# A later turn for the key's product in a planned schedule, and a third tile for the sample's state

## The chip, the cores and the metric

One core of a Trainium2 chip runs the whole program. The metric is the device time of one execution in microseconds (us); smaller is better. The profiled execution is one such execution, and its rows are what this document reads.

## The reference, cut to what matters

One inference step of a one-layer encoder over 512 prompt tokens and 32 sample tokens, each of width 1024. RMSNorm is followed by one wide input projection, three recurrent mixers (Mamba-2, GLA, RWKV-7), a gated merge, cross attention over 256 memory tokens, and a final norm. The change touches the RWKV-7 mixer, which is, for each of 16 heads with a 64 by 64 state S:

```
S_t = S_{t-1} diag(w_t) - (S_{t-1} kk_t)(kk_t * a_t)^T + v_t k_t^T
o_t = S_t r_t                # k7 = k7 * (1 + (a - 1) * k_a) is the key that enters as k_t
```

Prompt tokens start from a zero state, sample tokens from a given state, and both final states are outputs.

## The kernel before

All 544 tokens lie along the free axis and channels on 128 partitions. The big projections are sums of three float32 products with 128 by 128 weight blocks (tiles wh and wl against uh and ul, results in PSUM tiles pd): a block of weights is loaded by DMA into wraw, split into wh by ScalarE and wl by VectorE, and used by 48 matmuls. These dense blocks are also the filler for TensorE while a recurrence waits.

The RWKV mixer runs in eight iterations, one for each pair of heads, called 0 to 7 here. Tokens are cut into chunks of 64: chunks 0 to 7 are the prompt, chunk 8 the sample. One iteration passes through these generators:

- rw_A (preparation): from k, r and the decay to scaled operands on VectorE, ScalarE and GpSimd. GpSimd forms a factor (bk<-bk,dpar, L299) and from it the key k7, which lies in tile ks (ks<-ks,bk, L284). VectorE then forms bee (sq<-bk,GC), the key's product ka (bk<-ks,bk), kae (rn<-bk,GC) and rk (rs<-rs,par,ks). GpSimd copies a half of bk (bk<-bk, L305).
- rw_B: transposes tokens (ptk, copied by ScalarE to tm and t and from there by DMA into NK), multiplies bk with AR on TensorE (pp, 36 matmuls), masks them into NK, and stores parts to DRAM.
- rw_I: 31 steps of a small triangular inverse on GpSimd (im and td, 62 instructions).
- rw_J: two further block products of the inverse on TensorE (pW, then pT) with the ScalarE copy W between them.
- rw_C: the state chain, over chunk 8 first and then 0 to 7. In each chunk TensorE multiplies the state (pc<-Sb,AR), VectorE adds (R), TensorE solves (pc<-R,TT), VectorE writes NK (copy_predicated, L1198), TensorE multiplies again (pc<-NK), and VectorE updates the state (Sb<-Sb,GC,pc, or a plain copy in chunk 0, which has no state to start from).
- rw_N: the norm of the outputs.

Sb is a list of three tiles. The start state of the sample is loaded into Sb[2]. The new state of chunk c goes to Sb[c % 2], so chunk 8 writes Sb[0], which is also stored by DMA to the output (out_rwkv_s), and chunk 0 writes Sb[0] next.

The order of the instructions on every engine is fixed when the program is built. A planner (class Sched) keeps an estimated clock for every engine and an estimated finish for every region of a tile. Its generators run by priority; each appends instructions until it yields. A yielded number sends the generator to sleep until the planned clock of TensorE has advanced by that many nanoseconds; a yielded function, until it is true. `S.free("v")` is true once the planned VectorE is less than 900 ns ahead of TensorE; `S.at(x)` is the planned time that is left until x is written, on TensorE's clock, and zero when it is past. The chip does not see these clocks: it keeps the order and waits on semaphores. So a yield decides what stands ahead of an instruction in its engine's queue, not when it runs. The dense generator has the lowest priority and takes every turn that the others leave.

Many instructions come from helpers, and carry their lines: L284 is tensor_tensor, L293 scalar_tensor_tensor, L299 tensor_scalar, L305 copy, L278 activation, L245 matmul, L242 transpose, L327 DMA.

Of the kernel before, what the change touches and what calls it, by code (L numbers as in the profile page):

```python
# [46 lines left out]
       ("a", "v"): 145.0, ("a", "p"): 170.0, ("v", "a"): 130.0, ("v", "p"): 155.0, ("p", "v"): 70.0, ("p", "a"): 65.0,  # L47
       ("a", "q"): 150.0, ("v", "q"): 150.0, ("p", "q"): 150.0, ("v", "v"): 127.0, ("a", "a"): 153.0, ("p", "p"): 102.0}

W = dict(HOLD1=0, HOLD2=8, CALM=3000, EARLY1=1, DEPTH1=3, EARLY2=2, FAIR=1500, GRAIN=5, IS=900.0, IE=0, NQ=3000, XL=2, SG=6, PRW=800.0, R2=0.0, DE=2500.0, T2=0, FA=900.0, XM=3000.0, WARM=12)  # L50


class Cols:
# [72 lines left out]
class Sched:  # L126
# [22 lines left out]
    def run(self):  # L149
        idle = 0  # L150
        while self.threads:
# [4 lines left out]
            th = next(ready, None)  # L156
            if th is not None and th[0] >= 0 and self.n_small > W["FAIR"]:
                th = next((x for x in ready if x[0] == 9), th)
# [181 lines left out]
def body(tc, I, O):  # L340
    nc = tc.nc
    S = Sched(nc)
# [17 lines left out]
    with tc.manual_schedule(), \  # L360
# [447 lines left out]
        Sb = [rwp.tile([128, 2, 64], F32, name=f"Sb{i}") for i in range(3)]  # L808
# [80 lines left out]
        def ch(a):  # L889
            return a.rearrange("p (c t) -> p c t", t=64)  # L890
# [4 lines left out]
        def rw_A(p):  # L895
# [51 lines left out]
            bk = rwp.tile([128, 9, 3, 64], F32, name="bk", tag="bk")  # L947
# [35 lines left out]
            k7 = ks  # L983
# [3 lines left out]
            ar = d["AR"]  # L987
# [13 lines left out]
            bee = sq  # L1001
            gcol = d["GC"]
            S.cp(gcol, EE[:, :, 64:65])
            S.tt(ch(bee), be, gcol.to_broadcast([128, 9, 64]), MUL)
            yield S.free("v")
            S.tt(ka, ch(k7), Gi, MUL)
            yield S.free("v")
            kae = rn
# [9 lines left out]
        def rw_B(p):  # L1018

            yield has(f"rwK{p}", "rwR", f"vs{p}")  # L1020
            rk, vs, kae, bee, bk, d = hand.pop(p)
            ar = d["AR"]
            rwr = pools["rwR"][1]
            nk = d["NK"]

            def tokens(n_, src):

                yield S.at(src)
                ps = yield from bank("ptk")
                for i in range(4):  # L1030
                    S.mm(ps[:, i * 128:(i + 1) * 128], src[:, i * 128:(i + 1) * 128], C("ident"), True, True, transpose=True)
                tm = rwr.tile([128, 4, 128], F32, name="tm", tag="tm", bufs=TMB)
                yield S.since(tm, 1, "a") - S.t["pe"]
                S.act(tm.rearrange("p c t -> p (c t)"), ps[:, :512], AF.Copy)
                for i in range(2):
                    h = 64 * i
                    g = h if n_ == 2 else 64 - h
                    for r in range(2):
                        S.store(out=nk[g:g + 64, r:8:2, i, 1 if n_ else 3, :], in_=tm[r * 64:r * 64 + 64, :, h:h + 64])
                yield S.free("a")  # L1040

            yield from tokens(0, vs)

            yield S.at(bk, ar)
            for c0, cn in ((0, 4), (4, 4), (8, 1)):
                ps = []
                for _ in range(2):
                    ps.append((yield from bank("pp")))
                for c in range(cn):
                    for i in range(2):  # L1050
                        hs = slice(64 * i, 64 * i + 64)
                        S.mm(ps[i][:, c * 128:c * 128 + 128], bk[hs, c0 + c, i:i + 2, :].rearrange("p a t -> p (a t)"),
                             ar[hs, c0 + c], True, True)
                for i in range(2):
                    S.tt(nk[:, c0:c0 + cn, i, 0:3:2, :], ps[i][:, :cn * 128].rearrange("p (c a t) -> p c a t", c=cn, a=2),
                         two(C("m_rw")[:, 64 * i:64 * i + 128]).unsqueeze(1).to_broadcast([128, cn, 2, 64]), MUL)
                yield S.free("v")
            for i in range(2):
                S.store(out=rows64(n_scr[p % 2], i), in_=nk[i * 64:i * 64 + 64, :, i, 2 * i, :])
            done.add(f"rwN{p}")  # L1060

            r2 = rwp.tile([128, 2, TP], F32R, name="r2", tag="r2")
            rh, rl = r2[:, 0], r2[:, 1]
            parts(rk[:, :T], rh[:, :T], rl[:, :T])
            yield S.at(rl[:, :T], vs)
            for (o, w) in HV:
                ps = yield from bank("pbn")
                head_sums(ps[:, :w], rh[:, o:o + w], rl[:, o:o + w])
                S.tt(rk[:, o:o + w], ps[:, :w], vs[:, o:o + w], MUL)
                yield S.free("v")  # L1070
            S.store(out=b_scr[p], in_=rk[:, :T])
            done.add(f"rwB{p}")
            yield from tokens(1, kae)
            yield from tokens(2, bee)
            ps = yield from bank("ptk")
            for n_, (src) in enumerate((kae, vs, bee)):
                S.mm(ps[0:64, n_ * 128:n_ * 128 + 128], src[:, 512:576], C("ident"), True, True, transpose=True)
            t8 = rwr.tile([64, 3, 128], F32, name="t8", tag="tm", bufs=TMB)
            yield S.since(t8, 1) - S.t["pe"]
            S.act(t8.rearrange("p c t -> p (c t)"), ps[0:64, :384], AF.Copy)  # L1080
            for i in range(2):
                h = 64 * i
                S.store(out=nk[64 - h:128 - h, 8, i, 1:4:2, :], in_=t8[:, 0:2, h:h + 64])
                S.store(out=nk[h:h + 64, 8, i, 1, :], in_=t8[:, 2, h:h + 64])
            done.add(f"rwA{p}")
# [66 lines left out]
        IE = "pv"[W["IE"]]  # L1152
# [11 lines left out]
        def rw_C(p):  # L1164

            d = slot[p % NSLOT]
            yield has(f"rwA{p}")
            for i in range(2):
                S.dma(out=Sb[2][64 * i:64 * i + 64, i], in_=I["s0_rwkv"][64 * i:64 * i + 64, p])
            yield has(f"rwI{p}")  # L1170
            AR, NK, TTt, GC = (d[n_] for n_ in ("AR", "NK", "TT", "GC"))
            st_ = None
            yield S.stored(NK)
            yield S.at(Sb[2], NK, TTt)
            for c0, cn in ((4, 5), (0, 4)):
                ps = yield from bank("pr")
                for c in range(cn):
                    for i in range(2):
                        hs, gs = slice(64 * i, 64 * i + 64), slice(64 - 64 * i, 128 - 64 * i)
                        S.mm(ps[hs, c * 64:c * 64 + 64], NK[gs, c0 + c, i, 2 * i, :], NK[gs, c0 + c, i, 3, :], True, True)  # L1180
                S.act(NK[:, c0:c0 + cn, 0, 0, :], ps[:, :cn * 64].rearrange("p (c t) -> p c t", t=64), AF.Copy)
            NB = blocks8(NK)
            for c in [8] + list(range(8)):
                Ss = Sb[2] if c == 8 else (None if c == 0 else st_)


                pa = yield from bank("pc")
                pb = yield from bank("pc")
                pu = pa[:, 128:256]
                VU, R = NK[:, c, :, 3, :], both(NK[:, c, 0, 0, :])  # L1190
                if Ss is not None:
                    S.mm(pa[:, 0:128], AR[:, c].rearrange("p a t -> p (a t)"), Ss, True, True)
                    r_ = rwp.tile([128, 2, 64], F32, name="R", tag="R")
                    S.tt(r_, two(pa[:, 0:128]), R, ADD)
                    R = r_
                yield S.at(NK[:, c, 0, 0, :] if Ss is None else R)
                S.mm(pu, TTt[:, c, :], R, True, True)
                nc.vector.copy_predicated(VU, two(C("blk1").bitcast(I32)), two(pu))  # L1198
                S.note("v", 203, (VU,), (pu,))
                yield S.at(VU)  # L1200
                for i in range(2):
                    S.mm(pb[:, i * 64:i * 64 + 64], NK[:, c, i, 1 - i:3 - i, :].rearrange("p a t -> p (a t)"), VU[:, i, :], True, True)
                ns = Sb[c % 2]
                for i in range(2):
                    hs = slice(64 * i, 64 * i + 64)
                    if Ss is None:
                        S.cp(ns[hs, i], pb[hs, hs])
                    else:
                        S.stt(ns[hs, i], Ss[hs, i], GC[hs, c, :], pb[hs, hs], MUL, ADD)
                    if c >= 7:  # L1210
                        S.store(out=O["rwkv_s" if c == 8 else "rwkv_p"][hs, p], in_=ns[hs, i])
                st_ = ns
                yield S.at(ns)
                S.act(NB[:, c, 3:8:4, :], two(pb[:, 0:128]), AF.Copy)
                if Ss is not None:
                    S.act(NB[:, c, 0:7:6, :], two(pa[:, 0:128]), AF.Copy)
                else:
                    nc.gpsimd.memset(NB[:, c, 0:7:6, :], 0.0)
                    S.note("p", 200, (NB[:, c, 0:7:6, :],), ())
            done.add(f"rwC{p}")  # L1220
# [914 lines left out]
```

## Time and profile before

| what | value |
|---|---|
| median of three runs | 1309.08 us (1308.45 to 1312.62) |
| profiled execution | 1309.37 us |
| its span, first to last instruction | 1307.6 us |
| TensorE busy | 1266.1 us, 97% of the span |
| VectorE busy | 841.5 us, 64% |
| ScalarE busy | 624.7 us, 48% |
| GpSimd busy | 356.9 us, 27% |
| mean granted TensorE clock | 0.986 |

Busy times of different engines overlap. A granted clock of 1.00 is 2.4 GHz and one of 0.50 is 1.2 GHz; a figure between is the mean of a stretch that has both. The profiled execution's time is 1.8 us more than its span.

### The profile page before, as it was taken

The page shows a single profiled execution, that of the slowest core. Times are in us where ns is not written, and L with a number is a line of the kernel's source. Part 1 is how long each engine was busy: PE and PEld are TensorE (multiplying, and loading weights), DVE is VectorE, ACT ScalarE, POOL GpSimd, SP SyncE. Part 2 cuts the span into 40 slices and gives each one's busy share as a digit, 9 for nine tenths or more (in the row PEclk, how much of TensorE's full clock was granted, in tenths as well). Part 3 has the DMA queues.
Part 4 walks back from the last instruction along what each step waited for, and adds up shares of the span by engine and source line. Part 5 has one row for each costly group of instructions (what it writes and reads, how often), then busy time and mean ns, then how long its engine had stood idle before and what let it go on. Part 6 is the DMA issues. An engine that isn't in the chain of part 4 may idle for free.

```text
span 1307.6 us, 27538 instructions
## 1 busy us (share of the span) xinstructions
PE 1266.1 (97%) x10848; PEld 1219.7 (93%) x10848; DVE 841.5 (64%) x1666; ACT 624.7 (48%) x1191; POOL 356.9 (27%) x706
## 2 busy tenths in 40 slices
PE   8999989998999999999999999999999999999997
PEld 8999989998999888999999999888999999999997
DVE  6857875767685967554464878676665756575543
ACT  6565445455556363444555463634445323444422
POOL 0014845818372846520010533132000000000000
PEclk8999989999999998999999999999999999999999
DMA  8644455353535353633532442363886445440302
GB/s 293 194 121 117 121 140 124 104 135 114 125 93 141 105 132 111 161 108 131 173 136 70 138 125 95 111 187 98 289 317 239 137 133 189 171 146 25 106 17 69
DMA packets 170385, 181.11 MB, mean 139 GB/s; under 512 B 100480, under 2 KB 123104, under 8 KB 170128
## 3 DMA queue, kind: packets, MB, share of 16 engines
q1 hardware_dynamic: 169824, 178.68, 44.7%
q8 instruction: 86, 1.41, 0.4%
q10 hardware_dynamic: 432, 0.67, 0.2%
q14 instruction: 43, 0.35, 0.1%
HBM read 136.27 MB, written 35.39 MB: 131 GB/s over the span
## 4 chain that ended last, share of the span: by engine, by line
PE 56%; DVE 6%; POOL 5%; ACT 2%; DMA 2%; issue 2%; SPq 0%; POOLq 0%; DVEq 0%; ACTq 0%
PE pd L245 43%; PE pc L245 3%; POOL im L284 2%; POOL td L284 2%; PE psc L245 1%; PE pO L245 1%; PE py L245 1%; PE pov L245 1%; DVE wl L284 1%; PE pp L245 1%; PE ph L245 1%; PE pS L245 1%; PE pss L245 1%; PE pT L242 1%; ACT L278 0%
## 5 line engine op out<-in xcount | busy, mean ns | idle before, releaser
L245 PE MATMUL pd<-ul,wh 128*128 128x272 f32 (+1 forms) x1632 | 437.3, 296 | 0.0
L245 PE MATMUL pd<-uh,wh 128*128 128x272 f32 (+1 forms) x1632 | 432.5, 294 | 0.2 <-ACT wh L278 0.2
L245 PEld LDWEIGHTS pd<-ul,wh 128*128 128x128 f32 (+1 forms) x1632 | 309.3, 190 | 3.9 <-issue 2.2
L245 PEld LDWEIGHTS pd<-uh,wh 128*128 128x128 f32 (+1 forms) x1632 | 309.0, 189 | 3.8 <-issue 1.8
L245 PE MATMUL pd<-uh,wl 128*128 128x272 f32 (+1 forms) x1632 | 254.5, 293 | 3.0 <-DVE wl L284 3.0
L245 PEld LDWEIGHTS pd<-uh,wl 128*128 128x128 f32 (+1 forms) x1632 | 222.0, 190 | 6.9 <-DVE wl L284 4.2
L284 DVE TENSOR_TENSOR wl<-wraw,wh 128x1024 fp32r<-128x1024 f32 (+1 forms) x143 | 177.7, 1245 | 39.3 <-ACT wh L278 36.1
L278 ACT ACTIVATE wh<-wraw 128x1024 fp32r<-128x1024 f32 (+1 forms) x143 | 149.8, 1048 | 64.2 <-PE pd L245 38.0
L245 PE MATMUL pd<-uh,wr 128*128 128x256 f32 (+1 forms) x768 | 148.7, 291 | 1.4 <-ACT uh L278 1.4
L284 POOL TENSOR_TENSOR im<-td,nd 108x84 f32<-108x84 f32 (+23 forms) x248 | 117.5, 474 | 88.8 <-DMA td<-in_eye 48.2
L245 PEld LDWEIGHTS pd<-uh,wr 128*128 128x128 f32 x768 | 121.1, 188 | 2.9 <-ACT uh L278 1.6
L284 POOL TENSOR_TENSOR td<-td,im 108x84 f32<-108x84 f32 (+23 forms) x248 | 107.3, 433 | 19.4
L284 POOL TENSOR_TENSOR macc<-macc,hrs 128x288 f32<-128x288 f32 x3 | 2.3, 799 | 378.0 <-DVE macc L293 378.0
L245 PE MATMUL pd<-ul,wr 128*128 128x256 f32 (+1 forms) x384 | 100.5, 293 | 0.1
L245 PEld LDWEIGHTS pd<-ul,wr 128*128 128x128 f32 x384 | 72.4, 189 | 1.5 <-issue 0.8
L278 ACT ACT_TABLE_LOAD x55 | 70.6, 1283 | 1.4 <-DVE tB L284 0.5
L278 ACT ACTIVATE fg<-pd 128x272 f32<-128x272 f32 x64 | 24.9, 394 | 84.7 <-PE pd L245 79.8
L293 DVE SCALAR_TENSOR_TENSOR Sb<-Sb,GC,pc 64x64 f32<-64x64 f32 x128 | 35.7, 279 | 35.7 <-PE pc L245 33.7
L278 ACT ACTIVATE lerpA<-pd,par 128x272 f32<-128x272 f32 x50 | 24.3, 487 | 68.5 <-PE pd L245 56.4
L245 PE MATMUL pc<-NK 128*128 128x64 f32 x288 | 43.2, 273 | 5.8 <-DVE NK L1198 3.4
L278 ACT ACTIVATE NK<-pc 128x128 f32<-128x128 f32 x136 | 30.3, 273 | 37.9 <-DVE Sb L293 34.3
L278 ACT ACTIVATE fg<-pd,dpar 128x272 f32<-128x272 f32 x48 | 23.2, 486 | 50.2 <-PE pd L245 36.8
(469 smaller groups left out, 2421.0 us busy)
## 6 DMA issues: line engine op xcount, KB each, us to landing
wraw<-in_wall SPq DMA_DIRECT2D x165, 512.0 KB
g_mg<-fg SPq DMA_DIRECT2D x24, 272.0 KB
mgt<-g_mg SPq DMA_DIRECT2D x24, 272.0 KB
NK<-tm SPq DMA_DIRECT2D x96, 64.0 KB
ab<-acs_d SPq DMA_DIRECT2D x8, 512.0 KB
nd<-n_scr SPq DMA_DIRECT2D x24, 144.0 KB
n_scr<-NK SPq DMA_DIRECT2D x16, 144.0 KB
TT<-d_scr SPq DMA_DIRECT2D x16, 144.0 KB
```

What stands on the lines that cost most here:

```text
L242: self.nc.tensor.transpose(out, lhsT, rhs)
L245: self.nc.tensor.matmul(out, lhsT, rhs, start=start, stop=stop, skip_group_check=shared)
L278: self.nc.scalar.activation(out=out, in_=in_, func=f, scale=scale, bias=bias)
L284: eng.tensor_tensor(out=out, in0=a, in1=b, op=op)
L293: self.nc.vector.scalar_tensor_tensor(out=out, in0=a, scalar=s, in1=b, op0=op0, op1=op1)
```

## The change

Four edits. A new constant KM is 1500 ns. In rw_A the turn that was given up after bee is given up ahead of bee, and in its old place, ahead of ka, the generator sleeps until TensorE's planned clock is 1500 ns past the planned finish of k7 (or 1500 ns, if k7 is planned to be finished already). In rw_B the sleep ahead of the pp products is 1500 ns longer. In rw_C chunk 8 writes its new state to Sb[2] in place of Sb[0], over the start state that it has just read. No arithmetic instruction is added, removed or resized.

```
-W = dict(..., XM=3000.0, WARM=12)
+W = dict(..., XM=3000.0, WARM=12, KM=1500.0)
...
             gcol = d["GC"]
             S.cp(gcol, EE[:, :, 64:65])
+            yield S.free("v")
             S.tt(ch(bee), be, gcol.to_broadcast([128, 9, 64]), MUL)
-            yield S.free("v")
+            yield S.at(k7) + W["KM"]
             S.tt(ka, ch(k7), Gi, MUL)
             yield S.free("v")
             kae = rn
...
             yield from tokens(0, vs)
-            yield S.at(bk, ar)
+            yield S.at(bk, ar) + W["KM"]
             for c0, cn in ((0, 4), (4, 4), (8, 1)):
...
-                ns = Sb[c % 2]
+                ns = Sb[c % 2 if c < 8 else 2]
```

## Rows read from the trace of the kernel before

**Rows 1.** Windows: busy us (and count) of each engine, granted TensorE clock, DMA.
```profile
core 0: us, PE busy (x) PEld busy (x) DVE busy (x) ACT busy (x) POOL busy (x), PEclk, DMA share, GB/s
100.00:640.00 540.00, 516.38 (x4891) 495.32 (x4890) 355.45 (x743) 266.15 (x547) 273.97 (x574) 0.98 0.45 123
...
177.40:182.30 4.90, 4.90 (x51) 4.59 (x53) 4.14 (x6) 0.21 (x1) 1.73 (x3) 0.50 0.83 241
...
323.90:330.90 7.00, 7.00 (x42) 6.45 (x43) 4.52 (x12) 1.95 (x5) 5.14 (x17) 0.60 0.44 114
...
510.70:518.20 7.50, 7.49 (x44) 6.92 (x46) 3.49 (x8) 0.51 (x3) 2.76 (x8) 0.56 0.50 141
```

**Rows 2.** Waits of TensorE, 85 to 640 us: us in total, times, longest.
```profile
PE pc L245 <- DVE R L284: 5.4, 6, 2.6
PE pc L245 <- DVE Sb L293: 4.9, 2, 3.6
PE pT L245 <- ACT W L278: 3.5, 1, 3.5
...
PE pp L245 <- DVE lerpA L819: 1.0, 1, 1.0
...
PE pc L245 <- DVE Sb L305: 0.4, 1, 0.4
```

**Rows 3.** Waits of VectorE over the whole span.
```profile
DVE bk L284 <- POOL ks L284: 5.8, 2, 3.9
...
DVE Sb L305 <- DMA out_rwkv_s<-Sb: 1.6, 2, 1.3
```

**Rows 4.** Timeline of VectorE, iteration 4: start, length, instruction, [idle before].
```profile
316.75 0.30 DVE L1198 COPY_PREDICATED NK<-con,pc 128x128 f32<-128x128 int32 x1
320.95 0.76 DVE L284 TENSOR_TENSOR bk<-ks,bk 128x576 f32<-128x576 f32 x1 [3.90 <-POOL ks L284]
321.63 1.68 DVE L284 TENSOR_TENSOR wl<-wraw,wh 128x1024 fp32r<-128x1024 f32 x1
323.24 0.56 DVE L293 SCALAR_TENSOR_TENSOR Sb<-Sb,GC,pc 64x64 f32<-64x64 f32 x2
...
325.12 0.28 DVE L284 TENSOR_TENSOR R<-pc,NK 128x128 f32<-128x128 f32 x1
```

**Rows 5.** Timeline of GpSimd, iteration 4.
```profile
317.26 1.35 POOL L284 TENSOR_TENSOR yr<-yr,bo 128x544 f32<-128x544 f32 x1
318.60 0.82 POOL L299 TENSOR_SCALAR bk<-bk,dpar 128x576 f32<-128x576 f32 x1
319.50 1.41 POOL L284 TENSOR_TENSOR ks<-ks,bk 128x576 f32<-128x576 f32 x1
```

**Rows 6.** Timeline of TensorE, iteration 4.
```profile
314.35 0.38 PE L245 MATMUL pc<-Sb,AR 128*128 128x128 f32 x2
...
316.33 0.38 PE L245 MATMUL pc<-R,TT 128*128 128x128 f32 x2
...
323.86 0.79 PE L245 MATMUL pc<-Sb,AR 128*128 128x128 f32 x2 [3.59 <-DVE Sb L293]
```

**Rows 7.** Timeline of VectorE, iteration 7.
```profile
508.12 1.87 DVE L284 TENSOR_TENSOR bk<-ks,bk 128x576 f32<-128x576 f32 x1 [1.88 <-POOL ks L284]
510.02 0.44 DVE L293 SCALAR_TENSOR_TENSOR fg<-fg,pd 128x272 f32<-128x272 f32 x1
510.37 0.28 DVE L284 TENSOR_TENSOR R<-pc,NK 128x128 f32<-128x128 f32 x1
```

**Rows 8.** Timeline of TensorE, iteration 7.
```profile
506.64 0.38 PE L245 MATMUL pc<-Sb,AR 128*128 128x128 f32 x2
...
510.71 0.80 PE L245 MATMUL pc<-R,TT 128*128 128x128 f32 x2 [2.62 <-DVE R L284]
```

**Rows 9.** Tile bk: durations in ns, min/median/max, over the eight iterations.
```profile
L299 POOL TENSOR_SCALAR bk<-bk,dpar x8: 817/1073/2456, 96.9 to 505.8; 128x576 f32<-128x576 f32 x8
L284 POOL TENSOR_TENSOR ks<-ks,bk x8: 1406/1422/2279, 98.7 to 506.7; 128x576 f32<-128x576 f32 x8
```

**Rows 10.** Timeline of ScalarE, 168 to 180 us: the copy ahead of W.
```profile
176.58 0.48 ACT L278 ACTIVATE t<-ptk 64x384 f32<-64x384 f32 x1 [2.75 <-DMA NK<-tm]
```

**Rows 11.** Timeline of TensorE, 575 to 590 us: end of iteration 7's inverse, start of its chain.
```profile
579.90 0.69 PE L245 MATMUL pT<-TT,W 32*32 32x32 f32 x32
587.79 1.26 PE L245 MATMUL pr<-NK 64*64 64x64 f32 x36
```

More of the change, by code (lines that the diff above doesn't have):

```diff
@@ L48 @@
        ("a", "q"): 150.0, ("v", "q"): 150.0, ("p", "q"): 150.0, ("v", "v"): 127.0, ("a", "a"): 153.0, ("p", "p"): 102.0}
-W = dict(HOLD1=0, HOLD2=8, CALM=3000, EARLY1=1, DEPTH1=3, EARLY2=2, FAIR=1500, GRAIN=5, IS=900.0, IE=0, NQ=3000, XL=2, SG=6, PRW=800.0, R2=0.0, DE=2500.0, T2=0, FA=900.0, XM=3000.0, WARM=12)
+W = dict(HOLD1=0, HOLD2=8, CALM=3000, EARLY1=1, DEPTH1=3, EARLY2=2, FAIR=1500, GRAIN=5, IS=900.0, IE=0, NQ=3000, XL=2, SG=6, PRW=800.0, R2=0.0, DE=2500.0, T2=0, FA=900.0, XM=3000.0, WARM=12, KM=1500.0)
 class Cols:
@@ L1003, in rw_A @@
             S.cp(gcol, EE[:, :, 64:65])
+            yield S.free("v")
             S.tt(ch(bee), be, gcol.to_broadcast([128, 9, 64]), MUL)
-            yield S.free("v")
+            yield S.at(k7) + W["KM"]
             S.tt(ka, ch(k7), Gi, MUL)
@@ L1042, in rw_B @@
             yield from tokens(0, vs)
-            yield S.at(bk, ar)
+            yield S.at(bk, ar) + W["KM"]
             for c0, cn in ((0, 4), (4, 4), (8, 1)):
@@ L1202, in rw_C @@
                     S.mm(pb[:, i * 64:i * 64 + 64], NK[:, c, i, 1 - i:3 - i, :].rearrange("p a t -> p (a t)"), VU[:, i, :], True, True)
-                ns = Sb[c % 2]
+                ns = Sb[c % 2 if c < 8 else 2]
                 for i in range(2):
```

## Prediction

> **What bounds the kernel now.** I read the windows first, then the waits of TensorE and VectorE, then the timelines around the longest waits. In the stretch from 100 to 640 us, where the eight RWKV iterations run, TensorE is busy for 516.4 of 540 us [rows 1]. So TensorE is the bound there, and what an edit can win is in its 23.6 us of gaps and in the stretches in which its clock is granted at half. The waits say where the gaps lie: 4.9 us behind the state update Sb, 3.6 us of it at once; 5.4 us behind R, 2.6 us at once; 3.5 us in one wait for W [rows 2].
>
> Sb and R run on VectorE, so the next question is what VectorE did before them. It waited for GpSimd's key only twice, for 5.8 us together, the longer time for 3.9 us [rows 3]. The reader is to see that these two waits and the two longest TensorE gaps behind Sb and R are the same events. In iteration 4 VectorE is free at 317.05 (316.75 + 0.30) and stands before ka until 320.95, because GpSimd ends k7 at 320.91 (319.50 + 1.41) [rows 4, 5]. Behind ka in VectorE's queue wait a split wl and the state update Sb; Sb runs only at 323.24 [rows 4]. TensorE reaches the product with that state at 320.27 (323.86 - 3.59) and stands for 3.59 us [rows 6]. In iteration 7 VectorE waits 1.88 us, ka then takes 1.87 us, and R, queued behind it, starts at 510.37; TensorE stands for 2.62 us before the solve that reads R [rows 7, 8].
>
> Each gap costs twice. After the first the granted clock is 0.60 in the mean of the next 7.0 us, after the second 0.56 in 7.5 us, which mixes the levels 1.2 and 2.4 GHz; before both gaps TensorE was doing dense products without a break [rows 1]. If work goes in proportion to the clock, 7.0 x 0.40 = 2.8 us and 7.5 x 0.44 = 3.3 us of TensorE's time are lost there. So the two events cost 3.59 + 2.8 + 2.62 + 3.3 = 12.3 us.
>
> **The turn ahead of ka.** Nothing is added to any engine; the order changes. Before, only VectorE's planned backlog was asked for, so ka was appended while its input was still being made. Now at least 1500 ns of TensorE's planned time lie between bee and ka, and what the other generators append in that time stands ahead of ka.
>
> Iteration 4: TensorE's next steps were due within that time, so wl and Sb go first. VectorE does them from 317.05: 1.68 + 0.56 us [rows 4], ending at 319.3, before TensorE is there at 320.27. The 3.59 us gap and its 2.8 us go. What is late next is R, which now stands behind ka. GpSimd's k7 ends at 320.91 at best; at worst the wl beside it stretches it from 1.41 to the longest in the eight, 2.28 us [rows 9], to 321.8. With ka's 0.76 us and R's 0.28 us [rows 4], R ends between 322.0 and 322.8. TensorE wants it 1.98 us after its state product (316.33 - 314.35) [rows 6], at 322.25. So 0 to 0.6 us of wait comes back. I take 0.6, since GpSimd's operations in these rows do stretch.
>
> Iteration 7: fg and R go ahead of ka, so the solve is not held. ka starts at 508.12 as before and takes 0.76 [rows 4] to 1.87 us [rows 7], ending between 508.9 and 510.0. Late next is the predicated write after the solve: the state product is at 506.64 [rows 8], the solve 2.0 us later, its write at about 509.0. It is 0 to 1.0 us late. I take 1.0, as ka was as slow as that in this very place. Both returns are taken without a fall of the clock, which these rows show behind gaps of 2.6 and 3.6 us.
>
> In the other six iterations VectorE did not wait at ka [rows 3], so there the new turn wins nothing.
>
> **The turn ahead of pp.** VectorE's instruction before pp kept TensorE's pp waiting for 1.0 us once [rows 2]. With 1500 ns more between them that goes: -1.0 us, between 0 and -1.0. Everything after it is up to 1.5 us later, and with ka's turn up to 3.0 us in an iteration: the masks in NK, the stores and reloads that feed the inverse, GpSimd's 62 instructions, pW and pT, and SyncE's queue of the same transfers. I cost this at nothing. The work that hides it is dense filler, which TensorE has for this stretch [rows 1], and the start of the next state chain: in iteration 7 pT ends at 580.59 and the chain's first product starts at 587.79 [rows 11], 7.2 us later. If that cover were gone, the last chain would start up to 3.0 us later, once, since earlier delays are taken up by the chain that is still running. Bounds 0 and +3.0; I take 0.
>
> **The sample's state in Sb[2].** Chunk 0's copy no longer waits until the store of chunk 8's state has read Sb[0]: VectorE lost 1.6 us in two such waits [rows 3], and TensorE lost 0.4 us behind that copy [rows 2]. The same instructions run otherwise. The reload of Sb[2] for the next iteration must now wait for that store, but a whole chain of eight chunks lies between. -0.4 us, between 0 and -1.6.
>
> **Sum.** -12.3 + 0.6 + 1.0 - 1.0 - 0.4 = -12.1 us against the profiled 1309.37 us: 1297.3. That execution lies 0.3 us above the median shown, so 1297 for a median. A change under 0.3%, 3.9 us, can't be told from none for this kernel.
>
> **Rivals.**
>
> *GpSimd becomes later, so part of the wait stays.* While VectorE stood before ka, GpSimd ran alone. Now VectorE works beside it. The same factor took 0.82 us then and up to 2.46 us elsewhere, k7 1.41 and up to 2.28 us [rows 5, 9]: together 1.64 + 0.87 = 2.5 us later. In iteration 4 k7 is then at 323.4 and R at 324.4, 2.2 us late, and with the low clock's 2.8 us 5.0 of the 6.4 us come back: 1297.3 - 0.6 + 5.0 = 1301.7. If iteration 7 goes the same way, ka ends at 511.4, 2.4 us late, and with 3.3 us for the clock: 1301.7 - 1.0 + 5.7 = 1306.4. For it: the spread of these durations. Against it: in iteration 4 the order puts only one wl and a short Sb beside them. The Trainium skill speaks for this rival ("SBUF — State Buffer", section "SBUF: two separate sides"): an operation of VectorE with two SBUF inputs and a GpSimd operation that reads SBUF exclude each other for a whole instruction, instead of sharing. By that rule one wl of 1.68 us could set k7 back by 1.68 us rather than 0.87, which by the steps above makes 1.4 us of the 0.6 and 1298.1 of the sum; the trace agrees that the same GpSimd work takes up to three times as long at some places (2.46 against 0.82 us).
>
> *The gaps only move.* The sleep is measured on planned clocks, and GpSimd ran later than ka's place in the order assumed, by 3.9 us in iteration 4 [rows 3]; 1.5 us is less. Also, a different order after iteration 0 changes what meets what in all later ones. If two gaps like those removed appear elsewhere, the time is 1307 to 1311. Against it: the instructions that TensorE missed were the next to be appended, so a small shift is enough.
>
> *A slower kernel: the inverse's copy W held behind a transposed tile.* Once, ScalarE stood 2.75 us before the copy t, because DMAs still read the tile's buffer, and W was queued behind [rows 10]; TensorE stood for 3.5 us before pT [rows 2] and then ran 4.9 us at 0.50 [rows 1]: 3.5 + 2.45 = 6.0 us a time. The transposes of rw_B come later now, and so closer to the next inverse product. Two further such meetings cancel the gain (1309.3); from the third on the kernel is slower: -12.1 + 18.0 = +5.9, 1315.3. Against it: it happened once in eight iterations.
>
> **How the numbers follow.** The forecast has a chance of 0.50, with its own range 1290 to 1301. The first rival has 0.18 (1302 to 1306), the second 0.16, the slower one 0.16. Faster by over 0.3%, below 1305.2: 0.50 and 0.15 of the first rival, 0.65. Within 0.3%: the rest of it and the second, 0.19. Slower: 0.16. The range: at the low end the W gap is broken up by the new order too and nothing comes back, 1297.3 - 6.0 - 1.6 = 1289.7, so 1289. At the high end it holds both middle cases, 1311, and leaves out the slower one and a little below.
>
> **What would show it.** After: no wait of VectorE for GpSimd's key above 2 us with Sb or R queued behind it; wl and Sb ahead of ka in iteration 4, fg and R in iteration 7; no TensorE wait of over 2 us behind Sb or R; two low-clock stretches fewer; TensorE's gaps in the RWKV stretch down from 23.6 us to about 16; no wait of chunk 0's copy for the store. I am wrong if new waits of some microseconds stand before W, pp or another link, each with a low-clock stretch behind it, or if GpSimd's factor and key take over 2 us each.

## The result, and the profile after

The changed kernel takes 1315.91 us in the median of nine runs (1313.18 to 1321.01), the kernel before 1308.07 us (1304.44 to 1312.62): a ratio of 1.0057, with a 95% interval of 1.0039 to 1.0076. It is slower, and outside the predicted range. In a second session of runs the same program had 1.0024 (1.0008 to 1.0041), so its cost is 0.2 to 0.6%. The profiled execution took 1321.0 us, the slowest of the nine, with a span of 1319.2 us.

Windows of the changed kernel, cut so that they part the start, the RWKV iterations, the stretch behind them and the tail (columns as in [rows 1]):

```profile
0.00:100.00 100.00, 93.48 (x705) 91.74 (x706) 65.52 (x115) 62.99 (x103) 5.46 (x28) 0.95 0.62 199
100.00:640.00 540.00, 513.48 (x4846) 489.79 (x4845) 357.51 (x744) 264.56 (x545) 279.89 (x580) 0.98 0.45 122
640.00:1010.00 370.00, 364.67 (x2989) 348.12 (x2988) 243.79 (x444) 186.71 (x320) 73.86 (x96) 1.00 0.49 164
1010.00:1400.00 390.00, 299.53 (x2315) 292.38 (x2313) 174.61 (x364) 111.03 (x225) 2.29 (x3) 0.99 0.27 90
```

The same windows of the kernel before, but for the one in [rows 1]:

```profile
0.00:100.00 100.00, 95.53 (x722) 93.57 (x723) 67.53 (x118) 63.47 (x104) 7.54 (x29) 0.97 0.62 199
...
640.00:1010.00 370.00, 366.34 (x3021) 350.14 (x3020) 248.07 (x450) 188.31 (x320) 73.08 (x101) 1.00 0.51 167
1010.00:1400.00 390.00, 287.87 (x2222) 280.72 (x2220) 170.45 (x358) 106.75 (x220) 2.30 (x3) 0.99 0.26 84
```

Both programs run the same matmuls, so the last row is a balance: what TensorE has not done by 1010 us it does in the tail. The tail's busy time is 299.53 against 287.87 us, 11.7 us more, and the span is 11.6 us longer. The matmuls missing at each cut tell where: 17 by 100 us, 45 more by 640, 32 more by 1010. In the RWKV stretch TensorE was idle for 26.5 us instead of 23.6. The profile of the second session (span 1313.2 us) has 23.7 us there, as before, 2 matmuls fewer at the start, and 40 fewer between 640 and 1010, where its idle time is 6.25 us against 3.66. So the expected 12 us are missing in both, and where the loss lies differs.

Did the waits go that the change is about? Waits of VectorE over the whole span, answering to [rows 3]:

```profile
DVE x L1134 <- DMA TT<-d_scr: 6.5, 5, 4.0
...
DVE bk L284 <- POOL ks L284: 1.4, 2, 0.8
```

The wait for GpSimd's key fell from 5.8 to 1.4 us, and chunk 0's wait for the store is no longer listed. But there is a new first row: the wait for the reloaded inverse (TT<-d_scr) is 6.5 us; before it was 3.1 us, 1.8 at the longest. Waits of TensorE from 85 to 640 us, answering to [rows 2]:

```profile
PE pc L245 <- DVE NK L1199: 9.3, 4, 3.6
PE pc L245 <- DVE R L284: 8.6, 12, 1.7
PE pT L245 <- ACT W L278: 3.4, 1, 3.4
PE pp L245 <- POOL bk L305: 1.4, 1, 1.4
```

Sb is not among the waits of 0.4 us and more, and the longest wait for R is 1.7 us. In their place stand 9.3 us for NK, 3.6 at once. Iteration 4 shows both halves of this. Timeline of VectorE, answering to [rows 4]:

```profile
316.81 0.57 DVE L293 SCALAR_TENSOR_TENSOR Sb<-Sb,GC,pc 64x64 f32<-64x64 f32 x2
318.16 0.76 DVE L284 TENSOR_TENSOR bk<-ks,bk 128x576 f32<-128x576 f32 x1 [0.79 <-POOL ks L284]
...
327.17 0.29 DVE L284 TENSOR_TENSOR R<-pc,NK 128x128 f32<-128x128 f32 x1 [0.94 <-PE pc L245]
331.46 0.95 DVE L1134 STREAM_TRANSPOSE x<-TT 64x256 f32<-64x256 f32 x2 [4.00 <-DMA TT<-d_scr]
332.44 1.29 DVE L284 TENSOR_TENSOR NK<-pp,con 128x512 f32<-128x512 f32 x2
333.64 0.29 DVE L1199 COPY_PREDICATED NK<-con,pc 128x128 f32<-128x128 int32 x1
```

and of TensorE, answering to [rows 6]:

```profile
317.80 0.39 PE L245 MATMUL pc<-Sb,AR 128*128 128x128 f32 x2
...
321.68 0.49 PE L245 MATMUL pc<-R,TT 128*128 128x128 f32 x2 [1.17 <-DVE R L284]
...
333.99 0.66 PE L245 MATMUL pc<-NK 128*128 128x64 f32 x4 [3.60 <-DVE NK L1199]
```

Sb goes ahead of ka, as forecast, and the state product at 317.80 waits for nothing. Some 10 us later VectorE stands for 4.00 us before the transpose of the inverse, whose reload has not landed; the mask that writes NK is queued behind it, and TensorE stands for 3.60 us, one hundredth more than in the gap that was removed. In the 7 us after it, from 334.0, the granted clock is 0.58, as it was 0.60 behind the old gap. In iteration 7 the wait at ka is gone too (ka starts at 497.28 without one), and the gap behind R is 1.70 us instead of 2.62. It has a low clock behind it (the third column from the right):

```profile
497.00:502.00 5.00, 4.90 (x27) 4.71 (x28) 4.68 (x10) 0.73 (x3) 4.46 (x8) 0.70 0.68 217
```

These lengths are those of one execution. In the profile of the second session, which has the same order, the reload keeps VectorE waiting in iteration 4 for 0.96 and 0.35 us instead of 4.00, and TensorE stands for 0.86 us before that NK product (at 329.67) instead of 3.60; the waits for W are 4.2 us there, in two.

### The profile page after: what moved, and what is told of

Same layout as the page of the kernel before. It is cut to its first block, busy times and chain, and to the rows that moved or that the text cites. A ratio compares the mean times of both kernels' runs of the same rounds, so it can differ in the third digit from the quotient of the medians.

```text
span 1319.2 us, 27513 instructions
## 1 busy us (share of the span) xinstructions
PE 1271.1 (96%) x10848; PEld 1222.0 (93%) x10848; DVE 841.4 (64%) x1666; ACT 625.3 (47%) x1191; POOL 361.5 (27%) x706
## 3 DMA queue, kind: packets, MB, share of 16 engines
q8 instruction: 86, 1.41, 0.5%
## 4 chain that ended last, share of the span: by engine, by line
PE 62%; DVE 11%; POOL 11%; DMA 7%; ACT 4%; issue 4%; SPq 1%; POOLq 0%; DVEq 0%; ACTq 0%
PE pd L245 47%; POOL im L284 5%; POOL td L284 4%; PE pc L245 3%; DVE wl L284 2%; DMA wraw<-in_wall 1%; SPq L327 1%; DMA td<-in_eye 1%; PE psc L245 1%; DMA n_scr<-NK 1%; PE py L245 1%; PE pO L245 1%; PE pov L245 1%; ACT L278 1%; DVE AR L284 1%
## 5 line engine op out<-in xcount | busy, mean ns | idle before, releaser
L284 POOL TENSOR_TENSOR td<-td,im 108x84 f32<-108x84 f32 (+23 forms) x248 | 110.2, 445 | 19.4
L245 PEld LDWEIGHTS pc<-NK 128*128 128x128 f32 x288 | 38.4, 192 | 14.1 <-DVE NK L1199 5.7
```

The costliest lines, as they stand in the source:

```text
L245: self.nc.tensor.matmul(out, lhsT, rhs, start=start, stop=stop, skip_group_check=shared)
L284: eng.tensor_tensor(out=out, in0=a, in1=b, op=op)
```

## The experiments

Ratios are to the kernel before on the same chip in the same session, with the 95% interval; "order" is that of the instructions on all engines, fixed at build time.

**1. The parts.** The whole change again, then each edit alone:

```
# e2: the state tile alone                    # e4: the pp turn alone
-  ns = Sb[c % 2]                             -  yield S.at(bk, ar)
+  ns = Sb[c % 2 if c < 8 else 2]             +  yield S.at(bk, ar) + 1500.0
# e3: ka's turn alone
+  yield S.free("v")
   S.tt(ch(bee), be, ...)
-  yield S.free("v")
+  yield S.at(k7) + 1500.0
   S.tt(ka, ch(k7), Gi, MUL)
```

> The changed kernel once more, for a second profile: its profiled execution so far was at 1321.0 us the slowest of nine, median 1315.9. Redraw theory (the new order moves the gaps of TensorE to other links, as many as before): the same gaps in the RWKV stretch as in the first profile, 3.6 us before a product that reads NK in iteration 4's time and 3.1 us near 530 us, and a time 6 to 9 us above the kernel before. Start theory (part of the difference lies before the change, in the first 100 us): the gaps of the first 100 us are 2 us shorter than in the first profile, and the time 5 us less than that execution.

> Only the sample's state in its own tile. If this edit is harmless: 1307 to 1309 us, at most 1.6 us less. Redraw theory: the planner books the store's wait on VectorE's clock, so even this edit changes the order after iteration 0, and the time can lie anywhere between 1300 and 1318 us without a wait that names Sb.

> Only the turn given up ahead of ka (and the one moved ahead of bee). The prediction's mechanism: both gaps behind ka gone, 1296 to 1300 us. Redraw theory: those two gaps gone and others of 2 to 4 us in their place, 1305 to 1318 us.

> Only the 1500 ns ahead of the pp products. If the later pp products are what costs (the inverse starts later, its reload meets the state chain): 1314 to 1318 us with waits behind the reload of TT. If they cost nothing: 1307 to 1309 us. Redraw theory: anywhere between 1300 and 1318 us, with the wait at ka in some iteration still there.

Measured: whole 1.0024 (1.0008 to 1.0041), tile alone 1.0021 (0.9999 to 1.0044), ka alone 0.9966 (0.9939 to 0.9993), pp alone 0.9945 (0.9924 to 0.9967). The edit priced at 12 us brought a third of it, the one priced at 1 us more than that, and the sum of the three, -0.68%, is not the whole. The repeat came out 4.4 us above the kernel before in the median, less than the 6 to 9 expected with the same gaps, and without the 3.6 us gap; its first 100 us have 1.3 us less idle time than in the first profile, of the 2 expected by the other theory. Then in pairs:

> Both turns of 1500 ns, the sample's state as before. If the edits add up (ratios 0.9966 and 0.9945 alone): 1296 us, ratio 0.991. If the state's tile is what made the whole change slow (alone 1.0021): likewise 1296. Redraw theory: no sum; anywhere from 1297 to 1316 us, and the gaps in other places than in either alone.

> The turn ahead of ka with the state's tile, no turn ahead of pp. If the tile's edit costs in every company (0.2% alone, 0.9% beside both turns): 4 to 10 us above the ka turn alone, 1309 to 1315. Redraw theory: anywhere between 1298 and 1316, on either side of 1304.8.

> The turn ahead of pp with the state's tile, no turn ahead of ka. If the tile's edit costs in every company: 4 to 10 us above the pp turn alone, 1307 to 1313. Redraw theory: anywhere between 1298 and 1316, on either side of 1303.

Both turns without the tile: 0.994 (0.9915 to 0.9964). Ka and tile: 1.0015 (0.9991 to 1.0038); pp and tile: 1.0032 (1.0009 to 1.0056). By these ratios, adding the tile to one turn cost 0.5 and 0.9%, and to both 0.8 to 1.2%. That needs a cause of its own.

**2. Is it the tile, or the planner's book?** The store of chunk 8's state marks its source as read until a planned time. With the state in Sb[2], chunk 0's copy no longer meets that mark, the planner's clock of VectorE is earlier there, and every later decision can change. Two kernels take these apart: the tile on the chip with the mark still on the old tile, so that the order is that of before; and the old tile without the mark, which has the order of the tile alone:

```
# e9: Sb[2] as in the change, and                # e10: Sb[c % 2] as before, and
-  self.mark(in_, 1, "d", t)                     -  self.mark(in_, 1, "d", t)
+  self.mark(self.book.get(..., in_), 1, "d", t) +  if out.name != "out_rwkv_s":
   # the book has Sb[0] for the store of chunk 8  +      self.mark(in_, 1, "d", t)
```

> The sample's state in its own tile, while the planner books the store's end on the old tile, so that every engine's order is that of the kernel before. What the tile itself is worth on the chip. The prediction's term: VectorE's 1.6 us of waiting for the store is gone and the time falls by 0 to 1.6 us, 1307 to 1308.5. If the tile itself costs (its reload queued behind the store on SyncE): above 1311, as with the whole edit.

> The old tile, but the planner no longer books the end of the sample state's store, so that every engine's order is that of the kernel with the state's tile alone (1312.5). Order theory: 1311 to 1315 us, as slow as that kernel or up to 3 us slower, since chunk 0's copy now meets the store more often. Tile theory: 1307 to 1309.

The tile in the old order: 0.9994 (0.9968 to 1.002). The tile's order without the tile: 1.0046 (1.0023 to 1.0069). So the buffer itself costs and wins nothing that shows; the order that follows from it costs. The same with the whole change, its tile on the chip, and the mark where it was, which has the order of both turns without the tile:

> The whole change on the chip, tile included, but the planner books the end of the store on the old tile; every engine's order is that of the kernel with both turns alone. Booking theory: the ratio of that kernel, 0.992 to 0.996, so 10 us under the changed kernel. If the tile costs on the chip: 1.002 to 1.006.

0.9956 (0.9934 to 0.9978), against 0.994 for that order with the old tile and 1.0024 to 1.0057 for the change as written. Whether the change is faster or slower hangs on one kind of mark in the planner's book.

**3. Is a later mark better, or is any other order a draw?** Up to here all orders with the mark stood at 1.0002 or below, those without at 1.0015 or above (the runs of parts 1, 2 and 4). If the mark's time were good in itself, more of it should do no harm, and a fixed time in its place should help; if every shift deals a new order, the results should scatter:

```
# e14: the whole change; at chunk 0
+  if c == 0: S.t["v"] = max(S.t["v"], S.t["pe"] + 2000.0)
# e15: both turns, old tile (e16: the kernel before, with 100.0 in place of 1500.0)
-  self.mark(in_, 1, "d", t)
+  self.mark(in_, 1, "d", t + (1500.0 if out.name == "out_rwkv_s" else 0.0))
# e8: the whole change
-  KM=1500.0
+  KM=1600.0
```

> The whole change with 1600 ns in place of 1500. If the change has a cost or gain of its own, 100 ns in sixteen sleeps moves it by under 1.6 us: 1311 to 1316. Redraw theory: gaps in other places and a time that differs from the changed kernel's by several us either way, 1300 to 1320.

> The whole change; at chunk 0 the planner's VectorE clock is set at least 2000 ns past TensorE's, in place of the store's end. Booking theory (planned time at that place keeps filler in the state chain): 0.990 to 0.998. Draw theory: anywhere from 0.992 to 1.006, and no nearer to the booked orders than to the others.

> Both turns, the old tile, and the store's end booked 1500 ns later than before. Booking theory: 0.988 to 0.996, at least as good as both turns alone (0.994). Draw theory: 0.992 to 1.006.

> The kernel before with the store's end booked 100 ns later, so a new order with no edit of any weight. Booking theory: among the booked orders, 0.993 to 1.001. Draw theory: 0.992 to 1.006. Its distance from 1 is the size that an order alone can give.

Measured: 1.0022 (1.0007 to 1.0037), 0.9981 (0.9961 to 1.0), 1.0004 (0.9977 to 1.003), and for 100 ns on the planned end of the sample state's stores in the kernel before, nothing else changed, 1.0068 (1.0041 to 1.0094): the highest ratio of all. The theory of a mark that is good in itself has fallen. The windows of that kernel's tail show the same balance as the change's:

```profile
1010.00:1400.00 390.00, 298.15 (x2285) 290.69 (x2283) 177.87 (x370) 119.02 (x236) 2.29 (x3) 0.99 0.27 90
```

and its waits of TensorE, 85 to 640 us, are others again:

```profile
PE pc L245 <- DVE Sb L293: 8.0, 6, 4.5
PE pc L245 <- DVE R L284: 5.0, 8, 1.5
PE pc L245 <- DVE lerpA L819: 3.9, 2, 3.3
```

**4. The forecast's own mechanism.** Ka's turn in the two iterations alone in which VectorE waited (`yield S.at(k7) + 1500.0 if p == 7 else S.free("v")`, then with `p in (4, 7)`):

> The turn ahead of ka in iteration 7 alone, so that every engine's order up to 500 us is that of the kernel before. The prediction's step: R goes ahead of ka, the 2.6 us gap before the solve and its low clock (3.3 us) are gone, up to 1.0 us comes back; 1302 to 1304 us. Redraw theory: that gap is gone, but the order of the following 120 us is another; one more gap of 2 to 3 us with its low clock is as likely as not, and the time between 1301 and 1310.

> The turn ahead of ka in iterations 4 and 7 alone; the order up to 315 us is that of the kernel before. The prediction's step: both gaps gone, 1296 to 1299 us. Redraw theory: the gap near 320 us is gone, others of 2 to 4 us appear after it, 1300 to 1314 us.

1.0002 (0.9983 to 1.0022) and 0.9991 (0.9973 to 1.0009): nothing that can be told from noise. But e6 redraws the order from iteration 7 on. E7 has the order of e6 in all but ka's place in iteration 4 and seven matmuls next to it, so between these two the place of ka is all but alone, and it brings nothing clear of noise either. The last kernels keep the whole order of the kernel they are built on: the planner books ka at its old place, and its instruction alone is issued later on VectorE, right ahead of kae. In e17, built on the kernel before, this moves ka behind wl and Sb in iteration 4 and behind fg and R in iteration 7; every other instruction on every engine stands where it stood. E18 does it in all iterations of the kernel with the pp turn alone, which still had one wait of ka of 3.0 us.

```
-  S.tt(ka, ch(k7), Gi, MUL)
+  S.note("v", ..., (ka,), (ch(k7), Gi))             # booked here
   yield S.free("v")
+  nc.vector.tensor_tensor(out=ka, in0=ch(k7), ...)  # issued here; e17: if p in (4, 7)
   kae = rn
```

> The planner books the key's product at its old place, so that every engine keeps the order of the kernel before; on VectorE alone the instruction ka is issued two or three places later in iterations 4 and 7, right ahead of kae, behind wl and Sb in the one and behind fg and R in the other. This is the prediction's mechanism and nothing else. The prediction's own term (both gaps of TensorE behind ka's wait and their low clock go, 12.3 us, less 1.6 left): 1309 - 10.7 = about 1298, ratio 0.992. If only the gaps' own lengths go and the clock stays low: 6.2 - 1.6, about 1304.5, ratio 0.9965. If the gaps move to the next product that is late (the theory of the runs so far): 1306 to 1311, ratio 0.998 to 1.0015, with a TensorE wait for another tile of over 1.5 us where the two gaps were, or later in the same iteration.

> The order of the run with the turn at pp alone (ratio 0.9945), and in it the instruction ka issued right ahead of kae in every iteration, with every other engine's order kept. That run still had one wait of ka for ks of 3.0 us (at 494). The prediction's mechanism: that wait's gap goes, 3 us and its low clock, 5 to 6 us below the turn at pp alone, ratio about 0.990. If gaps only move: the ratio of the turn at pp alone, 0.993 to 0.996.

E17: 1.0 (0.9982 to 1.0018), 1307.91 us. The mechanism alone, with nothing redrawn, is worth nothing that can be measured. The trace of one execution shows where the win went. TensorE in iteration 4:

```profile
318.15 0.63 PE L245 MATMUL pc<-NK 128*128 128x64 f32 x4 [1.30 <-DVE NK L1204]
321.06 0.38 PE L245 MATMUL pc<-Sb,AR 128*128 128x128 f32 x2
...
325.94 0.63 PE L245 MATMUL pc<-NK 128*128 128x64 f32 x4 [0.87 <-DVE NK L1204]
...
331.81 0.62 PE L245 MATMUL pc<-NK 128*128 128x64 f32 x4
...
338.92 0.66 PE L245 MATMUL pc<-NK 128*128 128x64 f32 x4 [2.22 <-DVE NK L1204]
...
344.32 0.49 PE L245 MATMUL pc<-R,TT 128*128 128x128 f32 x2
```

and the same products in the kernel before:

```profile
335.79 0.63 PE L245 MATMUL pc<-NK 128*128 128x64 f32 x4
...
340.64 0.66 PE L245 MATMUL pc<-NK 128*128 128x64 f32 x4
...
344.55 0.49 PE L245 MATMUL pc<-R,TT 128*128 128x128 f32 x2
```

Sb's gap of 3.59 us is gone, and by 331.81 the chain is 3.98 us ahead of its old time (335.79). At the next NK product it is 1.72 us ahead (338.92 against 340.64), and at the solve after that 0.23 us (344.32 against 344.55). What took the first part of the lead is on VectorE:

```profile
315.68 2.12 DVE L284 TENSOR_TENSOR sq<-bk,GC 128x576 f32<-128x576 f32 x1
...
335.64 0.44 DVE L1139 STREAM_TRANSPOSE x<-TT 64x256 f32<-64x256 f32 x1 [0.18 <-DMA TT<-d_scr]
338.09 0.44 DVE L1139 STREAM_TRANSPOSE x<-TT 64x256 f32<-64x256 f32 x1 [2.01 <-DMA TT<-d_scr]
338.56 0.30 DVE L1204 COPY_PREDICATED NK<-con,pc 128x128 f32<-128x128 int32 x1
```

In the kernel before this pair of transposes starts at 339.36 and waits for nothing: the late Sb had hidden the late reload. The reload hardly moves with the chain: SyncE issues it at 332.44, and in the kernel before at 333.32. With Sb on time, VectorE comes to the transposes 3.7 us earlier, the second waits 2.01 us for the DMA, and the mask and TensorE (2.22 us) stand behind it. The rest of the lead went to the clock behind this new gap, first e17, then the kernel before, which has no gap there:

```profile
338.90:344.30 5.40, 5.38 (x54) 5.08 (x54) 2.97 (x9) 0.93 (x3) 0.00 (x0) 0.68 0.63 101
```

```profile
340.60:344.50 3.90, 3.90 (x55) 3.70 (x54) 2.41 (x8) 2.27 (x6) 0.00 (x0) 1.00 0.57 89
```

If work goes in proportion to the clock, as the forecast had it, 5.4 x 0.32 = 1.7 us are lost there (an estimate). Windows of this kernel and of the one before, 50 us around each of the two old gaps:

```profile
300.00:350.00 50.00, 45.02 (x424) 42.16 (x424) 36.83 (x82) 21.38 (x48) 28.99 (x59) 0.97 0.47 124
500.00:550.00 50.00, 47.21 (x483) 44.86 (x482) 33.52 (x68) 20.69 (x47) 26.62 (x55) 1.00 0.51 135
```

```profile
300.00:350.00 50.00, 45.74 (x426) 42.84 (x424) 35.76 (x84) 22.03 (x49) 29.11 (x60) 0.93 0.45 123
500.00:550.00 50.00, 47.38 (x469) 45.42 (x468) 31.97 (x67) 20.03 (x45) 26.52 (x55) 0.93 0.50 129
```

TensorE's idle time there is 4.98 + 2.79 = 7.8 us, against 4.26 + 2.62 = 6.9 us before: all of the idle time came back, in smaller pieces. In iteration 7 these are 0.96 us before pp, which waits for ka itself, 0.67 before a state product and 0.92 behind ScalarE's copy of NK. The low clock did go in part (0.93 to 0.97 and to 1.00). So iteration 4 keeps nothing of its lead, and iteration 7 some: the first product of its own chain (pr<-NK) starts at 586.12, 1.67 us ahead of [rows 11], and 0.21 us of that is older than the gap (499.69 against 499.90 at an NK product). The tail's busy time is 285.50 us against 287.87, 2.4 us less in these two profiled executions; the medians of 12 and 23 runs differ by 0.4 us.

E18: 0.9983 (0.9962 to 1.0005), where the kernel that it is built on had 0.9945 in an earlier session. It did not bring the 5 us of the forecast's mechanism. With the pp turn alone, ka's wait of 3.02 us held a mask, and TensorE stood for 4.31 us before the NK product at 496.49. Issued later, ka still waits 1.55 us (it starts at 498.45); kae is behind it, Sb behind kae, and TensorE stands for 3.49 us before the state product at 502.11. The gap went to another tile and lost 0.8 us. The ratio lies above both forecasts. The profile of e18 is 4.8 us longer than that of the pp turn alone, and ahead of this gap it is already 5.0 us behind (the state product at 493.06 stands at 488.05 there); what made that is open.

**Are the two gaps there in every execution?** Two more traces answer this. E6 has the order and the instructions of the kernel before up to iteration 7's ka. Yet in its iteration 4 ka does not wait, and no gap stands behind Sb. VectorE and then TensorE:

```profile
315.10 3.32 DVE L284 TENSOR_TENSOR AR<-rs,EE 64x576 f32<-64x576 f32 x2
...
320.64 1.02 DVE L284 TENSOR_TENSOR bk<-ks,bk 128x576 f32<-128x576 f32 x1
...
322.85 0.57 DVE L293 SCALAR_TENSOR_TENSOR Sb<-Sb,GC,pc 64x64 f32<-64x64 f32 x2
```

```profile
318.80 0.49 PE L245 MATMUL pc<-R,TT 128*128 128x128 f32 x2 [1.36 <-DVE R L284]
320.88 0.63 PE L245 MATMUL pc<-NK 128*128 128x64 f32 x4 [0.97 <-DVE NK L1200]
```

GpSimd was earlier there (yr starts at 315.13 instead of 317.26 [rows 5]) and ended the key at 319.69; VectorE's AR, beside yr, took 3.32 us instead of 1.60 in the kernel before, so VectorE came to ka after the key. E9 has the order of the kernel before throughout, with the state's tile. VectorE never waits for the key in it, and TensorE has neither gap; in iterations 4 and 7 it has these:

```profile
322.70 0.49 PE L246 MATMUL pc<-R,TT 128*128 128x128 f32 x2 [1.46 <-DVE R L285]
324.77 0.63 PE L246 MATMUL pc<-NK 128*128 128x64 f32 x4 [0.96 <-DVE NK L1199]
...
510.98 0.63 PE L246 MATMUL pc<-NK 128*128 128x64 f32 x4 [0.62 <-DVE NK L1199]
513.53 0.46 PE L246 MATMUL pc<-Sb,AR 128*128 128x128 f32 x2 [0.74 <-DVE Sb L294]
```

These executions were not 12 us faster for it: e9's took 1311.74 us, where the kernel before had a median of 1312.26 in that session, and e6's 1306.29 against 1308.59. TensorE's idle time from 100 to 640 us is 23.6 us in the kernel before, 24.3 in e9, 23.4 in e6 and 23.5 in e17.

## Why the prediction was wrong

- **TensorE is the bound, and the two waits at ka are the two long gaps.** Right of the execution that was read: its rows show it. But neither gap belongs to the order. With the same order, iteration 4 has no such gap in e6 and e9, and iteration 7 none in e9. So it is not shown that in e17 both went because ka was moved; in iteration 4 ka, though moved, still waited 0.84 us for the key, with wl and Sb now ahead of it.
- **What goes ahead of ka, and what is late next.** Nearly right. Sb (iteration 4) and fg and R (iteration 7) go ahead. R came out 1.17 and 1.70 us late in the two, against 0.6 taken and 1.0 for the predicated write. In iteration 7 the copy of GC took 1.31 and sq 1.86 us ahead of R, instead of 0.16 and 0.76. That is the stretching that the first rival named, on VectorE's side. Both returns were taken without a fall of the clock; behind the 1.70 us gap it fell, to 0.70 in 5 us, and behind the 1.17 us gap it did not (1.00 in the 5 us from 321.7).
- **The gaps and their low clock go: -12.3 us.** This is the step that failed, in two ways. The price was read from one execution and taken for what every execution of that order pays; e9, with that order and without these gaps, is no faster. And where ka is moved with the order held, e17 wins 0.4 us in the median, with an interval of 2.4 us to either side of nothing. The working followed the chain for one product past each gap and took what lay beyond as hidden. The second rival was right that the gaps move, and its time, 1307 to 1311, is nearer than the forecast's. It gave a sleep too short and a redrawn order as reasons. A redrawn order does change the time (e13, e16), but the gaps move without one: e17 has neither. In e17's iteration 4 VectorE had a second late input 15 us behind the first, the reload of the inverse; it landed at 338.1 in e17, and in the kernel before inside the time that the late Sb took up. Of the low clock's 6.1 us, 1.7 came back behind the new gap in iteration 4, by the estimate above; around iteration 7 e17's clock stands at 1.00, and 1.5 us of lead is what is left there.
- **The pp turn: -1.0 us, its lateness free.** TensorE's wait at pp for lerpA went, and one for GpSimd's bk, 1.4 us, came. Alone the edit gave -0.55%, seven times the price, with a new order of everything; no run separates the turn from its order. That lateness is free was not borne out in the change: the inverse's reload kept VectorE waiting for 6.5 us instead of 3.1. How much of it the later pp caused is open.
- **The state tile: -0.4 us.** The wait for the store went, and on the chip the tile is worth 0.9994 (0.9968 to 1.002), which agrees, and can't be told from nothing. The step overlooked that the planner prices the same wait. Taking it out of the book changes the order on all engines, and beside one turn or both that cost 0.5 to 1.2%. This is where the sign of the result comes from: the same change in the order with the mark ran at 0.9956.
- **The slower rival.** Wrong in its mechanism: the wait for W is 3.4 us, once, as before. That its time, 1315.3 us, lies near the measured 1315.9 is luck.

What the order does is shown to this point. The 18 runs hold 14 orders, if e17 and e18 are left aside; two of them are near copies (e7 of e6, and e8 of the change, from which it differs in some places between 258 and 299 us only). Where one order was timed twice, the two ratios differ by 0.06 to 0.33% (before and e9, e2 and e10, e5 and e13, the change and e1); the first three pairs differ by the tile on the chip too. Over the orders they go from 0.994 to 1.0068, and the mean of the 13 new ones, with pairs averaged, is 1.0004. So an edit that shifts a planned clock deals a new order from a spread of some 1.3%, of which a gap removed on paper says little. Which property makes an order good stays open: the two turns together are reliably fast (two kernels, 0.994 and 0.9956), but their waits show no single cause. What they do have is less idle time of TensorE from 100 to 640 us, 16.3 and 18.4 us, where the forecast had looked for about 16 as a sign of its own mechanism. No version beat them.

## What to carry to other kernels

Before a stall on a recurrence is priced, look for it in a second execution of the same program: here two gaps priced at 12 us stood in one and were missing in others of the same order. Then read on along the chain to the next place where a second input joins it, and see how early that input is: a gap is worth only the slack to the next late arrival, here a DMA reload 15 us further on. In a kernel whose order a planner makes, count an edit's effect on the planner's book as a change of its own: run it with the book held, and the book without it, and take the scatter of a few meaningless shifts as the error of any forecast.

## What the runs showed of the hardware

VectorE and GpSimd held each other up, by about the length of what the other was running. In e17 GpSimd's yr<-yr,bo ran from 315.82 for 1.35 us, and VectorE's sq, which starts at 315.68 in the rows, while GpSimd's td still runs (from 315.52 for 0.34 us), took 2.12 us: the 0.78 us that it took in the kernel before, and 1.34 us more, the length of yr. Then GpSimd's key took 2.29 us beside VectorE's wl, instead of 1.41 [rows 5]: 0.88 us more, where wl, at 317.92 for 1.64 us, overlaps its first 0.99 us. The Trainium skill says this of the port that the two share ("SBUF — State Buffer", section "SBUF: two separate sides"): it is an exclusive lock for a whole instruction, not a split of bandwidth. The trace agrees with that rule better than with a mere slowing (1.34 us for an instruction of 1.35, and 0.88 for an overlap of 0.99), and it holds for VectorE as the victim too, which the forecast's rival had left out.

The granted clock fell behind a shorter gap than the forecast had seen, 1.84 us before 475.50 in the kernel before:

```profile
475.50:480.50 5.00, 5.00 (x28) 5.00 (x29) 2.50 (x6) 2.89 (x8) 4.14 (x12) 0.66 0.49 139
```

but not behind the 0.87 us gap in e17's iteration 4, whose next 5 us, from 326.0, stand at 1.00. In the changed kernel it fell behind the 1.70 us gap and not behind the one of 1.17 us, as shown above.
